# A two-layer trunk in fp32: tile work moved from GpSimd to VectorE and ScalarE, and the norms' full outputs kept for the seven products

## The chip, the cores and the metric

One Trainium2 chip, one of its cores. The time is the device time of one execution in microseconds; several executions of each kernel are timed, and the median counts. A trace of one profiled execution goes with it. The engines are named PE (TensorE, matrix products), DVE (VectorE), ACT (ScalarE), POOL (GpSimd) and SP (SyncE, which issues the transfers). "L162" is line 162 of the kernel before; the lines of the changed kernel lie up to five away.

## The reference

An encoder trunk of two layers on 512 tokens of 1024 features. Each layer has three steps, so there are six in all, n = 0 to 5; each ends in a residual and a layer norm:

```python
for i in range(DEPTH):
    mods = (cond @ ada_w[i] + ada_b[i]).reshape(b, N_SUB, 3, D_MODEL)
    gate = lambda s: (1 + mods[:, s, 2])[:, None, :]
    y = swiglu(modulate(x, mods[:, 0]), ffn_w_gate[i, 0], ffn_w_up[i, 0], ffn_w_down[i, 0])
    x = layer_norm(ALPHA * x + 0.5 * gate(0) * y, ln_g[i, 0], ln_b[i, 0])
    u = modulate(x, mods[:, 1])
    ...
    x = layer_norm(ALPHA * x + gate(1) * y, ln_g[i, 1], ln_b[i, 1])
    y = swiglu(modulate(x, mods[:, 2]), ffn_w_gate[i, 1], ffn_w_up[i, 1], ffn_w_down[i, 1])
    x = layer_norm(ALPHA * x + 0.5 * gate(2) * y, ln_g[i, 2], ln_b[i, 2])
```

The middle step is a bidirectional Mamba-2 scan in layer 0 (n = 1) and differential attention in layer 1 (n = 4); n = 0, 2, 3, 5 are SwiGLU feed-forward networks (FFN) of width 2816. `modulate(x, m)` is x * (1 + scale) + shift, where shift, scale and gate come from the condition vector through the large matrix ada_w.

## The kernel before, in words

**Layout.** Activations lie transposed: features on the 128 partitions, the 512 tokens along the free axis, so x is eight tiles res[0] to res[7] of 128x512 fp32.

**Products.** An fp32 product is made of three matmuls in a reduced format (`mm3`, L158 to L166; all show as L162): each factor is split into a rounded part and the remainder, and hi x hi, hi x lo and lo x hi are summed. Inputs are uh and ul (or hi and lo for the inner activations), weights wh and wl. `load` fetches 128x1024 of weights to one of four buffers (raw); `split` (L102 to L121) makes the rounded part on ACT (L119, or L110) and the remainder on DVE (L120). In the form "a" it makes two tiles wah and two tiles wal of 128x512 in the pool "a", which holds NA tiles; of the two wal (L112) POOL makes the first and DVE the second, except in the start, where DVE makes both.

**The norm** (class LN, L260 to L361). `start` estimates the mean of each token from the first 128 features by a matmul with z0 (L272) and takes the estimate m0 off all eight res tiles (L277: six on DVE, two on POOL). `feed` adds each tile, as its residual is done (L371, DVE), to a running sum sc (L292) and its square (ACT, L288) to ss (L293); both sums are POOL's, but where a tile comes late (`late`) the sc sums and the last ss sum are DVE's. `stats` reduces sc and ss over the partitions on PE (L299, L303), makes 1/std (small DVE steps, a power on POOL at L317), spreads it on PE (L249, the broadcast) and takes the rest of the mean off on DVE (L321). `normalize` multiplies by 1/std (L347, DVE), makes uh and a full copy lt on ACT (L349, two ACTIVATEs per tile), and ul = lt - uh on DVE (L350). lt is a scratch tile. The scalings of res for the next residual (`residual`, L357, ACT) wait in the list `later`.

**The end of a step** (`down_units`, L388 to L417). All but the last four output blocks (six in n = 1 and 4) are made for all tokens. The last ones are kept and made by token halves, 256 columns each: the statistics and the normalising of the first half run while PE makes the second half's blocks. While the second half's statistics and normalising run, PE can work on the next layer's first products for the first token half. Their weights, the first units (`first_units`, L378 to L386: two or three units of 128x1024), are split in the form "a".

**The FFN.** In n = 2, 3 and 5 the blocks from f = 4 on are made by a scheme with seven half-size products in place of eight (`seven`, L476). It needs sums and differences of the full fp32 inputs: `input_forms` (L426 to L445) rebuilds each full input tile as uh + ul (L431, eight adds in an FFN), forms four sums for each pair of tiles (L433 to L436) and splits them. This goes on during f = 0 to 3. FFN 0 makes its blocks the plain way; it makes the forms near its end (f = 18 to 21) too, with eight adds, and doesn't use them. Between the blocks a stream of ada products runs (L180, DVE: one 128x1024 product with its sum per unit, with its own load through raw).

**The start** (L1031 to L1059). For each of the eight tiles d: two ada products on DVE, the shift and scale columns, uh and a full copy on ACT (L1045), ul on DVE (L1047; POOL for d = 0), the scaling of res by ALPHA on POOL (L1051), and the split of a weight unit, in the form "a" for d < 6.

**What sets the order.** Each engine works its own instructions in one fixed order, and waits by semaphores. That order isn't the program's: a scheduler fills the engines from the program, within the buffers that the pools have. A tile that is claimed from a pool comes behind the pool's tiles that the program claimed ahead of it. SP issues the loads in order.

Of the kernel before, what the change touches and what calls it, by code (L numbers as in the profile page):

```python
# [17 lines left out]
KT = D // P  # L18
FT = 22
FPARTS = (8, 7, 7)  # L20
NA = 32
NE = 5
NG = 4
NST = 128
# [22 lines left out]
def hybrid_trunk(tc, xT, cb, par, cst, adaw, wgu, wdn0, wdn1, wdn2, wdt, win, wso, wqk, wv, wao, dist_in, dtp, lam_in, out):  # L47
# [17 lines left out]
    def tmp(name="tmp"):  # L65
        return tp.tile([P, T], F32, tag="t", name=name)
# [28 lines left out]

    extra = [None]
    behind = []
    first_split = [True]
    first_ln = [None]
    turn = [0]  # L100

    def split(raw, where=None):  # L102

        n = raw.shape[-1]
        if where == "a":
            hi, lo = [], []
            for o in range(0, n, T):
                r = raw[:, o : o + T]
                h, l = big(F32R, "wah"), big(F32R, "wal")
                x = nc.scalar.activation(h, r, AF.Copy)  # L110
                eng = nc.vector if first_split[0] or o else nc.gpsimd
                y = eng.tensor_tensor(out=l, in0=r, in1=h.bitcast(F32), op=ALU.subtract)  # L112
# [147 lines left out]
    class LN:  # L260
# [6 lines left out]
        def start(self):  # L267

            pm = acc("ln")
            z0 = tp.tile([P, T], F32R, tag="t", name="z0")  # L270
            nc.scalar.activation(z0, res[0], AF.Copy)
            nc.tensor.matmul(pm, lhsT=onesn, rhs=z0, start=True, stop=True)  # L272
            m0 = ap.tile([P, T], F32, tag="l", name="m0", bufs=3)
            nc.scalar.activation(m0, pm, AF.Copy)
            for d in range(KT):
                eng = nc.gpsimd if d >= 6 else nc.vector
                eng.tensor_tensor(out=res[d], in0=res[d], in1=m0, op=ALU.subtract)  # L277
# [3 lines left out]
        def feed(self, d, a, b, late=False):  # L281
            z = res[d][:, a:b]
            if d == 0:
                self.start()
                nc.scalar.activation(self.ss[:, a:b], z, AF.Square)
                return
            sq = sp.tile([P, T], F32, tag="sq", name="sq")
            nc.scalar.activation(sq[:, a:b], z, AF.Square)  # L288
            c0 = res[0] if d == 1 else self.sc
            e0 = nc.vector if late else nc.gpsimd  # L290
            e1 = nc.vector if late and d == KT - 1 else nc.gpsimd
            e0.tensor_tensor(out=self.sc[:, a:b], in0=c0[:, a:b], in1=z, op=ALU.add)  # L292
            e1.tensor_tensor(out=self.ss[:, a:b], in0=self.ss[:, a:b], in1=sq[:, a:b], op=ALU.add)  # L293

        def stats(self, a, b):
            n, m = self.n, (b - a) // P
# [27 lines left out]
        def normalize(self, a, b, rb):  # L324
            n = self.n
            if n == 5:
                for d in range(KT):
                    t = res[d][:, a:b]
                    nc.vector.scalar_tensor_tensor(
                        out=t, in0=t, scalar=pc(C_LNG + n * 8 + d), in1=rb, op0=ALU.mult, op1=ALU.mult  # L330
                    )
                    nc.scalar.activation(t, t, AF.Identity, bias=pc(C_LNB + n * 8 + d))
                    if d % 2:
                        nc.sync.dma_start(
                            out[(d - 1) * P : (d + 1) * P, a:b].rearrange("(e p) t -> p e t", e=2),
                            resid[:, d - 1 : d + 1, a:b],
                        )
                return
            if self.u is None:
                self.u = [  # L340
                    tuple(ap.tile([P, T], F32R, tag="u", name=x, bufs=2 * KT) for x in ("uh", "ul")) for _ in range(KT)
                ]
            for d in range(KT):
                G, B = lnG[n][:, d : d + 1], lnB[n][:, d : d + 1]
                z, t = res[d][:, a:b], tmp("lt")[:, a:b]
                uh, ul = self.u[d][0][:, a:b], self.u[d][1][:, a:b]
                nc.vector.tensor_tensor(out=z, in0=z, in1=rb, op=ALU.mult)  # L347
                for o in (uh, t):
                    nc.scalar.activation(o, z, AF.Identity, bias=B, scale=G)  # L349
                nc.vector.tensor_tensor(out=ul, in0=t, in1=uh.bitcast(F32), op=ALU.subtract)  # L350
# [22 lines left out]
            op0=ALU.mult, op1=ALU.add,  # L373
        )

    next_u = [None]

    def first_units(n):  # L378

# [8 lines left out]
    def down_units(n, u, units, last, KEEP=4):  # L388
# [15 lines left out]
        if last:  # L404
            rbs = []
            for a, b in HALVES:
                for d, w in keep:
                    pd = acc()
                    proj(pd, w, u, cols=((a, b),))
                    add_res(d, pd, n, a, b)  # L410
                    ln.feed(d, a, b, late=True)
# [11 lines left out]

    def input_forms(u):  # L426

        for k in range(4):
            top, bot = tmp("ft"), tmp("fb")
            for o, d in ((top, k), (bot, k + 4)):  # L430
                nc.vector.tensor_tensor(out=o, in0=u[d][0].bitcast(F32), in1=u[d][1].bitcast(F32), op=ALU.add)  # L431
# [75 lines left out]
    def ffn(n, stream=None, per=(0, 0), pre=None, first7=FT):  # L507
# [6 lines left out]
        u = next_u[0]  # L514
        f = 0
        pre = pre or first_units(n)
        for pi, nf in enumerate(FPARTS):
            hs = []
            open7 = None
            for _ in range(nf):  # L520
# [19 lines left out]
                nc.vector.tensor_tensor(out=h, in0=sg, in1=pu, op=ALU.mult)  # L540
                hs.append(split_act(h))
                if first7 - 4 <= f < first7:
                    making = making or input_forms(u)
# [490 lines left out]
    for d in range(KT):  # L1034
# [20 lines left out]
    first_split[0] = False  # L1055
    behind.clear()
    next_u[0] = up
    st0 = ada_stream(0, range(16, 72))
# [111 lines left out]
```

## Time and profile before

| | |
|---|---|
| median of 3 runs | 2225.82 us (2225.81 to 2229.15) |
| profiled execution, its time | 2227.95 us |
| its span in the trace | 2226.2 us |
| PE, DVE, ACT, POOL busy | 97%, 76%, 47%, 12% of the span |
| granted PE clock, mean | 0.991 |
| matmuls / DVE / ACT / POOL instructions | 13030 / 2850 / 1758 / 332 |
| HBM read, written | 289.53 MB, 5.24 MB |

The profile is read like this. The page gives each engine's busy time and what ended its waits; a group is a line, an engine, an operation and its tiles, with count, busy time, mean of one in ns, and the idle time ahead of it with the instruction that ended it. Stretches give busy times between two moments and the clock that PE was granted (1.00 is full speed). The timeline gives single instructions with start and length. Instructions of DVE and ACT overlap a little at their ends, so that the pitch from one start to the next may be shorter than the length shown. The norms' first statistics (the first L299) stand at 375.9, 825.8, 1194.1, 1556.2, 1847.9 and 2202.1 us for n = 0 to 5.

### The profile page before, as it was taken

Reading aid. Unit: us, or ns where it says so; the run is one execution under the profiler, and the core shown is the slowest. Engines: PE = TensorE matmul, PEld = TensorE weight load, DVE = VectorE, ACT = ScalarE, POOL = GpSimd, SP = SyncE. Lnnn points to the kernel's source line nnn. Section 1 sums busy time; section 2 is a strip of 40 time slices with the busy share of each in tenths; the row PEclk is TensorE's granted clock in tenths of the full one; section 3 lists DMA queues with packets and bytes.
Section 4 is the critical chain, followed back from the end, with each engine's and each line's share of the span. In section 5 each row is a group of like instructions: output and inputs, shape, how many; then the busy total and the mean of one; then the engine's idle time right before and its main releaser. Section 6 shows DMA issues by size and latency. Waiting matters only on the chain.

```text
span 2226.2 us, 33653 instructions
## 1 busy us (share of the span) xinstructions
PE 2161.8 (97%) x13030; PEld 1862.6 (84%) x13030; DVE 1697.3 (76%) x2850; ACT 1055.2 (47%) x1758; POOL 273.4 (12%) x332
## 2 busy tenths in 40 slices
PE   7999999999999989999999999999999999999998
PEld 5788888866777679889898989899877778989897
DVE  6865568556766689989888998897766679959696
ACT  4422234757656537434355534344755556425253
POOL 2000003035332330000003000003000012000003
PEclk9999999999999999999999999999999999999999
DMA  8865562375445423545542273733211122323231
GB/s 300 283 210 175 181 200 80 96 184 150 136 132 156 119 70 107 193 156 184 166 133 92 92 253 103 238 106 122 68 57 52 53 67 67 115 75 116 84 117 46
DMA packets 88545, 296.97 MB, mean 133 GB/s; under 512 B 9536, under 2 KB 12992, under 8 KB 88384
## 3 DMA queue, kind: packets, MB, share of 16 engines
q1 hardware_dynamic: 88384, 294.81, 41.8%
q8 instruction: 102, 1.67, 0.3%
q14 instruction: 59, 0.48, 0.1%
HBM read 289.53 MB, written 5.24 MB: 132 GB/s over the span
## 4 chain that ended last, share of the span: by engine, by line
PE 48%; DVE 9%; issue 4%; ACT 3%; DMA 2%; POOL 1%; POOLq 0%; ACTq 0%; DVEq 0%; SPq 0%
PE acc L162 38%; PE mid L162 6%; DVE wl L120 1%; DMA raw<-in_wdn 1%; PE mid L938 1%; DVE raw L464 1%; PE ln L162 1%; DVE wl L455 1%; DVE raw L180 1%; DVE lo L150 1%; PE ln L249 1%; DMA raw<-in_adaw 1%; ACT wh L119 1%; DVE resid L277 1%; DVE resid L371 0%
## 5 line engine op out<-in xcount | busy, mean ns | idle before, releaser
L162 PE MATMUL acc<-hi,wh 128*128 128x512 f32 (+1 forms) x1488 | 506.0, 341 | 9.8 <-DVE resid L371 6.7
L162 PE MATMUL acc<-hi,wl 128*128 128x512 f32 (+1 forms) x1488 | 505.9, 340 | 1.1 <-DVE wl L455 1.1
L162 PE MATMUL acc<-lo,wh 128*128 128x512 f32 (+1 forms) x1488 | 504.9, 339 | 0.0
L162 PE MATMUL acc<-uh,wh 128*128 128x512 f32 (+1 forms) x1256 | 441.6, 352 | 0.3 <-ACT wh L119 0.3
L162 PE MATMUL acc<-ul,wh 128*128 128x512 f32 (+1 forms) x1256 | 439.5, 350 | 0.2 <-DVE ul L1047 0.2
L162 PE MATMUL acc<-uh,wl 128*128 128x512 f32 (+1 forms) x1256 | 438.2, 349 | 0.8 <-DVE wl L120 0.8
L119 ACT ACTIVATE wh<-raw 128x1024 fp32r<-128x1024 f32 (+1 forms) x234 | 238.6, 1025 | 392.3 <-PE acc L162 199.1
L120 DVE TENSOR_TENSOR wl<-raw,wh 128x1024 fp32r<-128x1024 f32 (+1 forms) x234 | 281.2, 1202 | 81.1 <-ACT wh L119 71.3
L162 PEld LDWEIGHTS acc<-hi,wh 128*128 128x128 f32 x1488 | 283.8, 191 | 46.2 <-DVE resid L371 6.5
L162 PEld LDWEIGHTS acc<-hi,wl 128*128 128x128 f32 x1488 | 284.1, 191 | 32.2 <-DVE wl L455 1.5
L162 PEld LDWEIGHTS acc<-lo,wh 128*128 128x128 f32 x1488 | 283.9, 191 | 31.0 <-DVE lo L150 1.0
L162 PEld LDWEIGHTS acc<-uh,wh 128*128 128x128 f32 x1256 | 237.4, 189 | 40.2 <-issue 9.2
L454 ACT ACTIVATE wh<-raw 128x1024 fp32r<-128x1024 f32 x162 | 170.8, 1059 | 207.5 <-DVE raw L464 105.2
L162 PEld LDWEIGHTS acc<-uh,wl 128*128 128x128 f32 x1256 | 237.6, 189 | 35.0 <-issue 3.9
L162 PEld LDWEIGHTS acc<-ul,wh 128*128 128x128 f32 x1256 | 237.8, 189 | 33.7 <-issue 4.4
L180 DVE SCALAR_TENSOR_TENSOR raw<-raw,cond 128x1024 f32<-128x1024 f32 x144 | 176.9, 1235 | 55.8 <-DMA raw<-in_adaw 55.4
L455 DVE TENSOR_TENSOR wl<-raw,wh 128x1024 fp32r<-128x1024 f32 x162 | 196.9, 1219 | 27.1 <-ACT wh L454 26.1
L371 DVE SCALAR_TENSOR_TENSOR resid<-acc,gv,resid 128x512 f32<-128x512 f32 (+1 forms) x172 | 113.0, 659 | 78.5 <-PE acc L162 78.2
L464 DVE TENSOR_TENSOR raw<-raw 128x512 f32<-128x512 f32 x216 | 148.1, 689 | 4.4
L112 POOL TENSOR_TENSOR wal<-raw,wah 128x512 fp32r<-128x512 f32 x13 | 19.7, 1517 | 951.7 <-ACT wah L110 655.5
L162 PE MATMUL mid<-uh,wh 128*128 128x256 f32 (+2 forms) x332 | 94.7, 286 | 0.9 <-DVE up L496 0.9
L162 PE MATMUL mid<-uh,wl 128*128 128x256 f32 (+2 forms) x332 | 93.9, 283 | 0.0
(269 smaller groups left out, 3824.8 us busy)
## 6 DMA issues: line engine op xcount, KB each, us to landing
raw<-in_wgu SPq DMA_DIRECT2D x176, 512.0 KB, 3.9
raw<-in_adaw SPq DMA_DIRECT2D x144, 512.0 KB, 4.6
raw<-in_wdn SPq DMA_DIRECT2D x64, 448.0 KB, 3.7
raw<-in_win SPq DMA_DIRECT2D x40, 512.0 KB, 3.6
raw<-in_wdn SPq DMA_DIRECT2D x32, 512.0 KB, 4.5
rw<-scr SPq DMA_DIRECT2D x32, 512.0 KB, 5.4
ch<-scr SPq DMA_DIRECT2D x32, 256.0 KB, 3.5
raw<-in_wso SPq DMA_DIRECT2D x16, 512.0 KB, 3.5
```

The lines of the kernel that those rows point to most:

```text
L119: nc.scalar.activation(hi[:, :n], raw, AF.Copy)
L120: nc.vector.tensor_tensor(out=lo[:, :n], in0=raw, in1=hi[:, :n].bitcast(F32), op=ALU.subtract)
L150: y = nc.vector.tensor_tensor(out=lo, in0=src, in1=hi.bitcast(F32), op=ALU.subtract)
L162: last = nc.tensor.matmul(o, lhsT=a, rhs=b, start=start and j == 0, stop=j == n - 1, skip_group_check=not start)
L180: nc.vector.scalar_tensor_tensor(out=raw, in0=raw, scalar=1.0, in1=cond, op0=ALU.mult, op1=ALU.mult, accum_out=mods[l][:, j : j + 1],)
L249: nc.tensor.matmul(o[:, j * P : (j + 1) * P], lhsT=cols[:, j : j + 1].broadcast_to([P, P]), rhs=ident, start=True, stop=True)
L277: eng.tensor_tensor(out=res[d], in0=res[d], in1=m0, op=ALU.subtract)
L371: nc.vector.scalar_tensor_tensor(out=res[d][:, a:b], in0=pd[:, a:b], scalar=gvec[n][:, d : d + 1], in1=res[d][:, a:b], op0=ALU.mult, op1=A ...
L454: nc.scalar.activation(x[0], r, AF.Copy)
L455: nc.vector.tensor_tensor(out=x[1], in0=r, in1=x[0].bitcast(F32), op=ALU.subtract)
L464: nc.vector.tensor_tensor(out=o, in0=x, in1=y, op=ALU.add)
L938: nc.tensor.matmul(ss[m], lhsT=a[r, c], rhs=b[r, :], start=j == 0, stop=j == 2)
```

## The change

No tile work stays on POOL in the splits, the start, the feeds and the norms: the wal of the splits, the subtractions of the mean, the sc and ss sums and ul of d = 0 go to DVE, and the scaling by ALPHA in the start goes to ACT through the list `later`. (POOL keeps the small power at L317 and some work elsewhere.) In n = 1, 2 and 4, whose next step is an FFN with seven products, `normalize` writes the full tile not to scratch but to a kept tile "uf" of the pool "a", and `input_forms` works on it directly, without the adds of L431. The pool "a" grows from 32 to 35 tiles.

```diff
-NA = 32
+NA = 35
...
                 x = nc.scalar.activation(h, r, AF.Copy)
-                eng = nc.vector if first_split[0] or o else nc.gpsimd
-                y = eng.tensor_tensor(out=l, in0=r, in1=h.bitcast(F32), op=ALU.subtract)
+                y = nc.vector.tensor_tensor(out=l, in0=r, in1=h.bitcast(F32), op=ALU.subtract)
...
             for d in range(KT):
-                eng = nc.gpsimd if d >= 6 else nc.vector
-                eng.tensor_tensor(out=res[d], in0=res[d], in1=m0, op=ALU.subtract)
+                nc.vector.tensor_tensor(out=res[d], in0=res[d], in1=m0, op=ALU.subtract)
...
-            e0 = nc.vector if late else nc.gpsimd
-            e1 = nc.vector if late and d == KT - 1 else nc.gpsimd
-            e0.tensor_tensor(out=self.sc[:, a:b], in0=c0[:, a:b], in1=z, op=ALU.add)
-            e1.tensor_tensor(out=self.ss[:, a:b], in0=self.ss[:, a:b], in1=sq[:, a:b], op=ALU.add)
+            nc.vector.tensor_tensor(out=self.sc[:, a:b], in0=c0[:, a:b], in1=z, op=ALU.add)
+            nc.vector.tensor_tensor(out=self.ss[:, a:b], in0=self.ss[:, a:b], in1=sq[:, a:b], op=ALU.add)
...
+            if a == 0:
+                keep = n in (1, 2, 4)
+                self.full = [big(name="uf") if keep else None for _ in range(KT)]
+                next_full[0] = self.full if keep else None
             for d in range(KT):
                 G, B = lnG[n][:, d : d + 1], lnB[n][:, d : d + 1]
-                z, t = res[d][:, a:b], tmp("lt")[:, a:b]
+                z, t = res[d][:, a:b], (self.full[d] or tmp("lt"))[:, a:b]
...
-    def input_forms(u):
+    def input_forms(u, full):
...
         for k in range(4):
-            top, bot = tmp("ft"), tmp("fb")
-            for o, d in ((top, k), (bot, k + 4)):
-                nc.vector.tensor_tensor(out=o, in0=u[d][0].bitcast(F32), in1=u[d][1].bitcast(F32), op=ALU.add)
+            if full is not None:
+                top, bot = full[k], full[k + 4]
+            else:
+                top, bot = tmp("ft"), tmp("fb")
+                for o, d in ((top, k), (bot, k + 4)):
+                    nc.vector.tensor_tensor(out=o, in0=u[d][0].bitcast(F32), in1=u[d][1].bitcast(F32), op=ALU.add)
...
-        eng = nc.gpsimd if d == 0 else nc.vector
-        y = eng.tensor_tensor(out=hl[1], in0=uf, in1=hl[0].bitcast(F32), op=ALU.subtract)
+        y = nc.vector.tensor_tensor(out=hl[1], in0=uf, in1=hl[0].bitcast(F32), op=ALU.subtract)
...
-        nc.gpsimd.tensor_scalar(out=res[d], in0=res[d], scalar1=ALPHA, scalar2=None, op0=ALU.mult)
+        later.append(lambda d=d: nc.scalar.activation(res[d], res[d], AF.Copy, scale=ALPHA))
```

The instructions stand in another order after it. On PE, at the end of step 1 (the scan), where the second half's statistics are made; acc<-lo,wh and acc<-hi,wl are step 1's own last products, acc<-uh,wah, acc<-ul,wah and acc<-uh,wal those of FFN 2's first units. Before:

```order
L162 MATMUL acc<-hi,wl 128x256
L162 MATMUL acc<-uh,wah 128x256 x3
L162 MATMUL acc<-uh,wh 128x256
L299 MATMUL mid<-sc,onesd 128x256
L303 MATMUL ln<-invd,sc 128x1 x2
L303 MATMUL ln<-invd,ss 128x1 x2
L162 MATMUL acc<-ul,wah 128x256
L162 MATMUL acc<-uh,wal 128x256
L162 MATMUL acc<-uh,wah 128x256
L162 MATMUL acc<-ul,wah 128x256
L162 MATMUL acc<-uh,wal 128x256
```

and after:

```order
L160 MATMUL acc<-hi,wl 128x256
L294 MATMUL mid<-sc,onesd 128x256
L298 MATMUL ln<-invd,sc 128x1 x2
L298 MATMUL ln<-invd,ss 128x1 x2
L247 MATMUL ln<-csts,rr 128x128 x2
L160 MATMUL acc<-uh,wah 128x256
L160 MATMUL acc<-ul,wah 128x256
L160 MATMUL acc<-uh,wal 128x256
```

Before, four matmuls of the next FFN stand ahead of the statistics and 45 between them and the broadcast (ln<-csts,rr, L249, which comes behind the rows shown). After, the broadcast (now L247) follows the statistics directly, and the next FFN's matmuls come behind it.

On ACT, at the same place, the splits of the first units (wah, six tiles) before:

```order
L110 ACTIVATE wah_7287<-raw_7285 128x512
L110 ACTIVATE wah_7291<-raw_7285 128x512
L119 ACTIVATE wh_6908<-raw_6906 128x1024
L271 ACTIVATE z0_6866<-resid_88 128x512
L110 ACTIVATE wah_7297<-raw_7295 128x512
L274 ACTIVATE m0_6869<-ln_6865 128x512
L119 ACTIVATE wh_6914<-raw_6912 128x1024
L285 ACTIVATE ss_6880<-resid_88 128x512
L110 ACTIVATE wah_7301<-raw_7295 128x512
```

and after, first between the two halves' normalising (uh and uf), then at the end of it:

```order
L348 ACTIVATE uf_7182<-resid_88,lnB1_2254,lnG1_2252 128x256
L348 ACTIVATE uh_7173<-resid_88,lnB1_2254,lnG1_2252 128x256
L109 ACTIVATE wah_7279<-raw_7277 128x512
L348 ACTIVATE uh_7159<-resid_88,lnB1_2254,lnG1_2252 128x256
L348 ACTIVATE uf_7175<-resid_88,lnB1_2254,lnG1_2252 128x256
```

```order
L348 ACTIVATE uh_7173<-resid_88,lnB1_2254,lnG1_2252 128x256
L348 ACTIVATE uf_7182<-resid_88,lnB1_2254,lnG1_2252 128x256
L109 ACTIVATE wah_7283<-raw_7277 128x512
L356 ACTIVATE resid_88<-resid_88,lnab1_2259,lnag1_2257 128x512
L109 ACTIVATE wah_7289<-raw_7287 128x512
L356 ACTIVATE resid_88<-resid_88,lnab1_2259,lnag1_2257 128x512
L109 ACTIVATE wah_7293<-raw_7287 128x512
L117 ACTIVATE wh_7432<-raw_7430 128x1024
L109 ACTIVATE wah_7299<-raw_7297 128x512
```

Before, four of the six wah stand around the mean's estimate (z0, m0), ahead of all the normalising. After, the first stands behind the first half's 16 ACTIVATEs, and the others behind the second half's 16, in turn with the scalings of res (L356). Norms 2 and 4 show the same; norms 0 and 3 keep matmuls of the next step between the second statistics and the broadcast.

More of the change, by code (lines that the diff above doesn't have):

```diff
@@ L97, in hybrid_trunk @@
     behind = []
-    first_split = [True]
     first_ln = [None]
@@ L275, in start, with feed @@
             for d in range(KT):
-                eng = nc.gpsimd if d >= 6 else nc.vector
-                eng.tensor_tensor(out=res[d], in0=res[d], in1=m0, op=ALU.subtract)
+                nc.vector.tensor_tensor(out=res[d], in0=res[d], in1=m0, op=ALU.subtract)
             self.sc = ap.tile([P, T], F32, tag="l", name="sc", bufs=3)
             self.ss = ap.tile([P, T], F32, tag="l", name="ss", bufs=3)
-        def feed(self, d, a, b, late=False):
+        def feed(self, d, a, b):
             z = res[d][:, a:b]
@@ L374, in add_res @@
         )
-    next_u = [None]
+    next_u, next_full = [None], [None]
     def first_units(n):
@@ L410, in down_units @@
                     add_res(d, pd, n, a, b)
-                    ln.feed(d, a, b, late=True)
+                    ln.feed(d, a, b)
                 if rbs:
@@ L513, in ffn @@
         idx = {0: 0, 2: 1, 3: 2, 5: 3}[n]
-        u = next_u[0]
+        u, full = next_u[0], next_full[0]
         f = 0
@@ L542, in ffn @@
                 if first7 - 4 <= f < first7:
-                    making = making or input_forms(u)
+                    making = making or input_forms(u, full)
                     forms.append(next(making))
@@ L1054, in hybrid_trunk @@
     nc.sync.dma_start(csts, cst[:, : 2 * P].rearrange("p (j q) -> p j q", j=2))
-    first_split[0] = False
     behind.clear()
```

## The prediction

> **What bounds the kernel now.** I read the page first, then the busy times in chosen stretches, then groups of instructions, and last the timeline around the norms.
>
> ```profile
> PE 2161.8 (97%) x13030; PEld 1862.6 (84%) x13030; DVE 1697.3 (76%) x2850; ACT 1055.2 (47%) x1758; POOL 273.4 (12%) x332
> ```
>
> TensorE (PE) is busy for 97% of the span, so whatever the change does can only count where PE waits. The stretches tell where that is (columns: start and end, length, busy time of each engine, granted clock, DMA share, GB/s).
>
> ```profile
> 809.00:826.00 17.00, 13.34 (x93) 12.77 (x93) 15.71 (x22) 7.76 (x15) 12.85 (x11) 0.90 0.22 77
> 838.00:852.70 14.70, 13.77 (x105) 12.96 (x106) 14.11 (x42) 12.64 (x26) 0.71 (x1) 1.00 0.03 5
> 863.00:933.00 70.00, 68.62 (x509) 65.13 (x509) 68.75 (x114) 34.97 (x52) 0.00 (x0) 1.00 0.45 144
> 1167.00:1194.00 27.00, 22.79 (x143) 20.35 (x142) 25.72 (x28) 7.91 (x14) 18.29 (x13) 1.00 0.53 173
> 1193.80:1200.60 6.80, 6.54 (x29) 6.39 (x30) 4.00 (x14) 1.52 (x3) 0.74 (x2) 0.50 0.01 2
> 1209.40:1219.00 9.60, 9.45 (x78) 9.19 (x77) 8.62 (x29) 8.86 (x17) 0.71 (x1) 1.00 0.01 2
> 1533.50:1556.20 22.70, 22.67 (x143) 20.50 (x143) 16.36 (x21) 7.32 (x12) 14.77 (x11) 1.00 0.33 114
> 1830.00:1848.00 18.00, 13.91 (x95) 13.31 (x96) 16.67 (x23) 8.19 (x15) 12.65 (x10) 0.91 0.28 89
> 1859.00:1872.60 13.60, 13.57 (x112) 13.30 (x111) 12.87 (x38) 11.41 (x23) 0.86 (x2) 1.00 0.01 2
> 1880.00:1940.00 60.00, 60.00 (x458) 57.70 (x457) 57.62 (x95) 34.12 (x52) 0.00 (x0) 1.00 0.30 96
> 2100.00:2150.00 50.00, 50.00 (x416) 49.61 (x416) 43.71 (x67) 24.69 (x37) 0.00 (x0) 1.00 0.31 98
> ```
>
> Three things stand here. The last row is the steady state: 416 matmuls in 50 us, 0.12 us for one of 256 columns. The rows from 809, 1167 and 1830 are the first parts of norms 1, 2 and 4: PE idles 3.7, 4.2 and 4.1 us while DVE is nearly full (15.71 of 17, 25.72 of 27, 16.67 of 18) and POOL works beside it; the granted clock is 0.90 and 0.91 on the mean of the first and third, which is some 3.4 us at half speed, and 0.50 for 6.8 us behind the wait in norm 2. The rows from 838, 1209.4 and 1859 are the second halves of the same norms, and there PE is full: it works on the next layer's first units (wah and wal) while ACT and DVE normalise. This second overlap is what I think the change takes away.
>
> **The POOL work that goes to DVE.** The groups (mean ns after the busy time) price it.
>
> ```profile
> L277 DVE TENSOR_TENSOR resid<-resid,m 128x512 f32<-128x512 f32 x36 | 38.6, 1138 | 4.1 <-ACT m L274 4.1
> L431 DVE TENSOR_TENSOR fb<-uh,ul 128x512 f32<-128x512 f32 x16 | 10.9, 684 | 0.0
> L110 ACT ACTIVATE wah<-raw 128x512 fp32r<-128x512 f32 x38 | 22.0, 616 | 0.3 <-DMA raw<-in_wqk 0.3
> ```
>
> The same two-input DVE operation on 512 columns takes 1138 ns in L277, where POOL runs, and 684 ns in L431, where it doesn't. So DVE slows down for POOL's sake, and taking POOL's part over costs DVE less than it looks: 8 subtractions at 0.61 us (a pitch shown below) are 4.9 us, where 6 take 6 x 1.14 = 6.8. The Trainium skill ("SBUF — State Buffer", Who interferes with whom) says that a DVE instruction with two SBUF inputs contends with a GpSimd instruction that reads SBUF, whichever starts first holding the shared ports for a whole instruction. The two DVE rows agree; by that rule alone the first parts of the norms shorten and the total falls.
>
> How much sooner the first statistics come I worked out for norm 1, from rows of DVE in the start and in this norm (start, length; the pitch is from one start to the next).
>
> ```profile
> 18.57 1.10 DVE L112 TENSOR_TENSOR wal<-raw,wah 128x512 fp32r<-128x512 f32 x1
> ...
> 24.95 1.10 DVE L112 TENSOR_TENSOR wal<-raw,wah 128x512 fp32r<-128x512 f32 x1
> 25.97 1.21 DVE L180 SCALAR_TENSOR_TENSOR raw<-raw,cond 128x1024 f32<-128x1024 f32 x1
> ...
> 27.11 0.68 DVE L112 TENSOR_TENSOR wal<-raw,wah 128x512 fp32r<-128x512 f32 x1
> 27.72 1.21 DVE L180 SCALAR_TENSOR_TENSOR raw<-raw,cond 128x1024 f32<-128x1024 f32 x1
> ...
> 809.88 2.79 DVE L277 TENSOR_TENSOR resid<-resid,m 128x512 f32<-128x512 f32 x2 [2.02 <-ACT m L274]
> ...
> 820.58 0.47 DVE L371 SCALAR_TENSOR_TENSOR resid<-acc,gv,resid 128x256 f32<-128x256 f32 x1
> 820.98 0.56 DVE L292 TENSOR_TENSOR sc<-sc,resid 128x256 f32<-128x256 f32 x1
> ...
> 825.25 0.41 DVE L292 TENSOR_TENSOR sc<-sc,resid 128x256 f32<-128x256 f32 x1
> 825.59 1.48 DVE L293 TENSOR_TENSOR ss<-ss,sq 128x256 f32<-128x256 f32 x1
> ```
>
> The pitches are 0.61 for 512 columns (27.11 to 27.72), 1.14 for 1024 (25.97 to 27.11), 0.40 for a half-width residual (820.58 to 820.98), 0.34 for a half-width sum (825.25 to 825.59). After the change DVE has 8 x 0.61 for subtractions, 0.7 for one full residual, 1.14 for one wl, 2 x 0.61 for full sums, 6 x 0.40 and 12 x 0.34: 14.4 us. From 809.3 (half a microsecond sooner, an estimate: m0 no longer follows ACT work for the first units) that ends at 823.7, against 825.59 + 1.48 = 827.07 now: 3.4 us. I take 3.5. It could be no more than the 3.7 us of idle PE plus half of the 3.4 us at half clock, 5.4. In norm 2 the same ceiling is 4.2 + 3.4 = 7.6, in norm 4 it is 4.1 + 1.7 = 5.8. Between 0.65 of the ceiling, as in norm 1, and all of it I take 5.5 and 4.7; norm 2 in the lower part, because an ada product with its own load stands in its chain.
>
> **What the kept inputs move.** Each full tile uf is claimed from the pool that wah and wal use, ahead of them in the program. The order shows the effect: in norms 1, 2 and 4 the first wah stands behind all 16 normalising ACTIVATEs of the first half, the other five behind the 16 of the second half, and between the second half's statistics and the broadcast of 1/std PE has no next-layer matmul left (45, 17 and 45 of them before). Norms 0 and 3, which keep nothing, have their matmuls still there. After the broadcast PE can do what the first wah/wal pair allows, 12 matmuls (29 in norm 2, where a third product's 17 stand ahead too), and then waits for the second pair. When that is ready, R, follows from when the last normalising ACTIVATE of the second half ends now:
>
> ```profile
> 853.94 0.59 ACT L349 ACTIVATE uh<-resid,lnB,lnG 128x256 fp32r<-128x256 f32 x1
> 854.43 0.59 ACT L349 ACTIVATE lt<-resid,lnB,lnG 128x256 f32<-128x256 f32 x1
> ...
> 1222.68 0.59 ACT L349 ACTIVATE lt<-resid,lnB,lnG 128x256 f32<-128x256 f32 x1
> ...
> 1875.56 0.59 ACT L349 ACTIVATE lt<-resid,lnB,lnG 128x256 f32<-128x256 f32 x1
> ```
>
> Less the lead, plus 0.6 for wah (616 ns) and 0.6 for wal on DVE: R is 855.0 - 3.5 + 1.2 = 852.7 in norm 1, 1223.3 - 5.5 + 1.2 = 1219.0 in norm 2, 1876.15 - 4.7 + 1.2 = 1872.65 in norm 4. DVE arrives at the same moment: from the broadcast it has 16 half-width operations, six sums of the seven products that now stand among them, one ada product of 1.14 and two wal, 9.5 us, and ACT has 16 x 0.49 (853.94 to 854.43) + 1.2 = 9.0, a little after DVE's first product.
>
> What before has done by R, the windows that start with the second statistics count. 14 of each are the statistics' and the broadcast's own passes; 4, 14 and 4 next-layer matmuls stand ahead of the window. So it is 105 - 14 + 4 = 95, 78 - 14 + 14 = 78 and 112 - 14 + 4 = 102, against 12, 29 and 12: PE is behind by 83, 49 and 90 matmuls of 0.12 us, 10.0 + 5.9 + 10.8 = 26.7 us. After R the other pairs follow faster than PE eats them (24 matmuls, 2.9 us, for each pair; 1.5 us of ACT with a residual scaling between), so nothing more is lost.
>
> **The clock.** PE then idles several microseconds in each of the three norms. The half-speed stretches above followed such waits and lasted 3.4 or 6.8 us, which loses 1.7 or 3.4. I take 2.6 for each norm, 7.8.
>
> **The start.** In the rows of DVE above, one step of the chain (weight units of one d) takes 24.95 - 18.57 = 6.38 us. The wal beside POOL's scaling takes 1.10, the other 0.68; without POOL some 0.33 to 0.4 goes from each of six steps. ACT takes the eight scalings, between its wah's, where it waits for the chain anyway. I take -2.0 (between 6 x 0.4 = 2.4 and nothing).
>
> **The removed sums.** 24 of 32 adds of L431 go, 24 x 0.684 = 16.4 us of DVE. They stand in the first part of FFNs 2, 3 and 5, where PE is busy 68.62 of 70 us (863, FFN 2) and 60 of 60 (1880, FFN 5): PE hides them. I cost that at nothing; were the cover gone, it would be worth at most the 1.4 us of idle PE in the first of these. Norms 0, 3 and 5 lose POOL too, but there PE doesn't wait for DVE (1533.5, the first part of norm 3: PE 22.67 of 22.7, DVE 16.36); I take 0, at most -2 for the three. NA alone moves nothing in time.
>
> **The sum.** 26.7 + 7.8 - 2.0 = +32.5 us. On the profiled run (span 2226.2, run 2227.95) that is 2260.4; that run lies 2.1 above the median of 2225.82, so the forecast for the median is 2258.
>
> Its bounds: with leads of 2 us more in each norm (-6), no clock loss (-7.8), -0.4 in the start and -2 in the other norms it is +16; with half the leads (+6.9), 3.4 of clock in each norm (+2.4), a half-clock stretch more in norm 2 (+3.4) and no gain in the start (+2) it is +47. The forecast's own range is 2242 to 2273.
>
> **The rivals.** A: the freed DVE decides, the late splits are covered after all. For it speaks DVE's 1138 against 684 ns, against it PE's full rows from 838, 1209.4 and 1859, which no other work can fill. The gain is the leads and the start: 3.5 + 5.5 + 4.7 + 2.0 = 15.7, 2210. The Trainium skill ("GPSIMD Engine Reference", 4.1 Engine selection) would have it so: elementwise work on two tiles belongs on VectorE. Chance 0.05.
>
> B: slower only by the bare chain of the statistics, which the leads pay back. Norm 5 shows this chain with nothing in its way:
>
> ```profile
> 2212.87 0.28 PE L162 MATMUL acc<-hi,wl 128*128 128x256 f32 x1
> ...
> 2217.57 1.07 PE L249 MATMUL ln<-csts,rr 128*128 128x128 f32 x4 [1.90 <-POOL rr L317]
> ```
>
> 2217.57 - 2212.87 = 4.7 us. If PE went on at full pace right behind the broadcast, three norms would lose 14.1 and gain 13.7 + 2.0: 2224, no change. It decides if the second wah is ready with the broadcast, and the order of ACT speaks against that. Chance 0.07.
>
> C: more than forecast. The first units' loads keep three of four raw buffers until their splits, so the loads behind them come late as well. A load takes
>
> ```profile
> raw<-in_wgu SPq DMA_DIRECT2D x176, 512.0 KB, 3.9
> ```
>
> 3.9 us; two of them bare in each norm are 23, 2281. Against it: DMA is busy for 0.45 and 0.30 in the stretches from 863 and 1880, and PE has 144 matmuls, 17 us, to cover them. Chance 0.08.
>
> **How the numbers follow.** Forecast 0.80, A 0.05, B 0.07, C 0.08. A difference of 0.2%, 4.5 us, is about what a measurement of this kernel can tell. Faster 0.05 (A), same 0.07 (B), slower 0.88. The range reaches from a little below the forecast's own low end to C, 2236 to 2284; it leaves out A, B and the tails.
>
> **What would show it.** In the profile after, PE should idle twice in norms 1, 2 and 4: from the second statistics to the broadcast (some 5 to 6 us), and, after 12 matmuls (29), until the second wal; the granted clock should read 0.50 behind it. L277's subtractions on DVE should take some 0.65 us, and the first statistics come 3 to 5 us sooner in the norm. The beginnings of FFNs 2, 3 and 5 should stay full. It is wrong if PE has next-layer matmuls in that gap, if those norms take no longer than before, or if the loss is spread over the FFNs.

## The result and the profile after

The changed kernel takes 2250.51 us (median of 4 runs, 2245.99 to 2253.47), the kernel before 2227.49 on the same chips; the ratio is 1.0102, 95% interval 1.0081 to 1.0122. It is slower by some 23 us, where the forecast had 32.5 (2258); the time lies inside the range on record. The profiled run took 2250.82 us, its span 2249.0, 22.8 us more than the span before. The rows below are of that run, where no other is named.

First the page's engines, then stretches with the columns as before: the first part of norm 1; norm 1 from the second statistics to the broadcast, from there until the second wal, and a little on; the beginning of FFN 2; then norm 2 and norm 4 from the second statistics on, two stretches each, and a longer one behind the broadcast of norm 4.

```profile
PE 2164.1 (96%) x13030; PEld 1866.4 (83%) x13030; DVE 1689.1 (75%) x2924; ACT 1060.3 (47%) x1766; POOL 133.5 (6%) x226
```

```profile
803.00:818.40 15.40, 13.44 (x104) 12.81 (x104) 14.46 (x31) 5.27 (x10) 0.00 (x0) 1.00 0.14 49
828.50:835.00 6.50, 2.28 (x10) 2.10 (x10) 6.19 (x21) 6.50 (x14) 0.69 (x1) 0.54 0.02 4
835.00:846.90 11.90, 5.22 (x18) 4.13 (x18) 11.67 (x33) 10.92 (x23) 0.00 (x0) 0.50 0.12 44
846.90:849.50 2.60, 2.60 (x13) 2.54 (x13) 2.60 (x8) 2.60 (x5) 0.00 (x0) 0.51 0.54 200
858.00:928.00 70.00, 70.00 (x536) 67.25 (x535) 55.73 (x84) 32.94 (x49) 0.00 (x0) 1.00 0.39 129
1205.50:1210.20 4.70, 1.50 (x11) 1.37 (x11) 4.60 (x17) 4.70 (x11) 0.69 (x1) 0.75 0.00 2
1210.20:1219.60 9.40, 4.86 (x19) 4.08 (x19) 9.08 (x25) 8.53 (x18) 0.00 (x0) 0.50 0.00 0
1863.80:1870.40 6.60, 1.50 (x11) 1.37 (x11) 6.29 (x21) 6.60 (x14) 0.70 (x1) 0.71 0.00 0
1870.40:1882.00 11.60, 4.98 (x18) 4.09 (x18) 11.38 (x31) 10.62 (x22) 0.00 (x0) 0.50 0.15 46
1870.40:1892.00 21.60, 14.98 (x81) 13.83 (x82) 20.15 (x48) 20.47 (x36) 0.00 (x0) 0.61 0.36 119
```

In the second halves, where PE was full before, it now does 10 or 11 matmuls (the statistics' own) in 4.7 to 6.6 us, and some 18 in the next 9 to 12 us, while DVE and ACT are nearly full. The granted clock falls to 0.50 within the first stretch of each norm and stays there through the second. The beginning of FFN 2 is as full as it was (70 of 70; 68.62 before), with DVE at 55.73 in place of 68.75 us.

The timeline of PE in norm 1 (start, length, idle time and what ended it) shows the waits and what ended them; the last row is the power on POOL:

```profile
828.50 0.79 PE L294 MATMUL mid<-sc,onesd 128*128 128x256 f32 x2 [2.55 <-DVE sc L287]
...
835.05 1.22 PE L247 MATMUL ln<-csts,rr 128*128 128x128 f32 x4 [4.27 <-POOL rr L312]
836.72 0.58 PE L160 MATMUL acc<-uh,wah 128*128 128x256 f32 x1 [0.45 <-ACT wah L109]
...
841.83 0.58 PE L160 MATMUL acc<-uh,wal 128*128 128x256 f32 x1 [4.32 <-DVE wal L110]
...
846.19 0.58 PE L160 MATMUL acc<-uh,wah 128*128 128x256 f32 x1 [1.86 <-ACT wah L109]
```

```profile
834.30 0.69 POOL L312 TENSOR_TENSOR rr<-vr,mhalf 128x2 f32<-128x2 f32 x1 [12.71 <-DVE vr L308]
```

PE waits 4.27 us for the power on POOL with nothing else to do. The power itself takes 0.69; most of the wait is DVE's, whose small steps ahead of the power (up to 834.13) stand among the normalising of the first half. PE then does two matmuls with the first wah, waits 4.32 us for the first wal, does the ten that are left of the twelve, and waits 1.86 us for the second wah. That one comes on ACT right behind the last normalising ACTIVATE (uf at 845.04), and its wal on DVE ends at 846.91. The third row of DVE below is the second wal of norm 4, which ends at 1882.23. The weights are not what is late: SP issued the loads of the first two units from 799.13 on, they took some 3.4 us to land, and the first wah begins at 836.06.

```profile
799.13 2.08 SPq L93 DMA_DIRECT2D raw<-in_wgu  x2
```

```profile
836.06 0.61 ACT L109 ACTIVATE wah<-raw 128x512 fp32r<-128x512 f32 x1
...
845.04 0.58 ACT L348 ACTIVATE uf<-resid,lnB,lnG 128x256 f32<-128x256 f32 x1
845.53 0.61 ACT L109 ACTIVATE wah<-raw 128x512 fp32r<-128x512 f32 x1
```

```profile
841.10 0.68 DVE L110 TENSOR_TENSOR wal<-raw,wah 128x512 fp32r<-128x512 f32 x1
...
846.23 0.68 DVE L110 TENSOR_TENSOR wal<-raw,wah 128x512 fp32r<-128x512 f32 x1
...
1881.55 0.68 DVE L110 TENSOR_TENSOR wal<-raw,wah 128x512 fp32r<-128x512 f32 x1
```

Where the time came from is read by the same instruction in both runs. The remainder of the inner activations (L150, in the changed kernel L148) runs 192 times in either; the 1st, 46th, 71st, 106th, 111th, 161st and 181st lie in the first FFN, just ahead of norm 1, in FFN 2, at the end of FFN 3 (ahead of norm 3), in the attention behind norm 3, ahead of norm 4 and in FFN 5. Before:

```profile
63.54 0.68 DVE L150 TENSOR_TENSOR lo<-h,hi 128x512 fp32r<-128x512 f32 x1
802.53 1.13 DVE L150 TENSOR_TENSOR lo<-yn,hi 128x512 fp32r<-128x512 f32 x1
1114.64 0.69 DVE L150 TENSOR_TENSOR lo<-sg,hi 128x512 fp32r<-128x512 f32 x1
1529.34 0.69 DVE L150 TENSOR_TENSOR lo<-sg,hi 128x512 fp32r<-128x512 f32 x1 [0.70 <-ACT hi L149]
1609.19 0.69 DVE L150 TENSOR_TENSOR wtl<-ln,wth 128x512 fp32r<-128x512 f32 x1
1814.59 0.69 DVE L150 TENSOR_TENSOR wtl<-ln,wth 128x512 fp32r<-128x512 f32 x1 [0.18 <-ACT wth L149]
2028.09 0.68 DVE L150 TENSOR_TENSOR lo<-sg,hi 128x512 fp32r<-128x512 f32 x1
```

and after:

```profile
59.89 0.68 DVE L148 TENSOR_TENSOR lo<-h,hi 128x512 fp32r<-128x512 f32 x1
797.25 0.68 DVE L148 TENSOR_TENSOR lo<-yn,hi 128x512 fp32r<-128x512 f32 x1
1118.41 0.68 DVE L148 TENSOR_TENSOR lo<-sg,hi 128x512 fp32r<-128x512 f32 x1
1538.98 0.69 DVE L148 TENSOR_TENSOR lo<-sg,hi 128x512 fp32r<-128x512 f32 x1 [0.70 <-ACT hi L147]
1618.24 0.68 DVE L148 TENSOR_TENSOR wtl<-ln,wth 128x512 fp32r<-128x512 f32 x1
1823.69 0.69 DVE L148 TENSOR_TENSOR wtl<-ln,wth 128x512 fp32r<-128x512 f32 x1 [0.18 <-ACT wth L147]
2050.59 0.68 DVE L148 TENSOR_TENSOR lo<-sg,hi 128x512 fp32r<-128x512 f32 x1
```

The differences are -3.65, -5.28, +3.77, +9.64, +9.05, +9.10 and +22.50 us. So the start gained 3.7 and the way to norm 1 another 1.6; norm 1, with the beginning of FFN 2, cost 9.1, norm 2, with FFN 3, cost 5.9, norm 3 gave 0.6 back, and norm 4 cost 13.4. The three norms that keep their outputs make the whole loss, 28.3 us.

### The profile page after: what moved, and what is told of

Same layout as the page of the kernel before. It is cut to its first block, busy times and chain, and to the rows that moved or that the text cites. A ratio compares the mean times of both kernels' runs of the same rounds, so it can differ in the third digit from the quotient of the medians.

```text
span 2249.0 us, 33533 instructions
## 1 busy us (share of the span) xinstructions
PE 2164.1 (96%) x13030; PEld 1866.4 (83%) x13030; DVE 1689.1 (75%) x2924; ACT 1060.3 (47%) x1766; POOL 133.5 (6%) x226
## 4 chain that ended last, share of the span: by engine, by line
PE 76%; DVE 10%; ACT 4%; issue 4%; DMA 3%; POOL 2%; POOLq 0%; ACTq 0%; SPq 0%; DVEq 0%
PE acc L160 63%; PE mid L160 7%; DMA raw<-in_adaw 2%; DVE raw L178 1%; DVE raw L467 1%; PE mid L941 1%; DMA raw<-in_wdn 1%; POOL E L780 1%; PE ln L160 1%; DVE wl L118 1%; DVE wl L458 1%; PE mid L791 1%; ACT uh L348 1%; PE ln L247 1%; ACT uf L348 1%
## 5 line engine op out<-in xcount | busy, mean ns | idle before, releaser
L312 POOL TENSOR_TENSOR rr<-vr,mhalf 128x2 f32<-128x2 f32 x12 | 8.4, 696 | 1580.4 <-DVE vr L308 1219.3
```

## Experiments

The theory is that the claims make the loss: uf is claimed from the pool "a" ahead of wah and wal, so the splits of the next FFN's first units come behind the normalising, and PE has nothing to do meanwhile. Rival 1 is that the work moved from POOL to DVE costs; rival 2 that the kept tiles cost as such, whoever claims first. Ratios are to the kernel before on the same chip, with 95% intervals.

### The first units claimed ahead of the kept tiles (claim)

```diff
                 keep = n in (1, 2, 4)
+                if keep:
+                    next_pre[0] = first_units(n + 1)
                 self.full = [big(name="uf") if keep else None for _ in range(KT)]
...
-        pre = pre or first_units(n)
+        pre, next_pre[0] = pre or next_pre[0] or first_units(n), None
```

> The changed kernel with one edit: the first units of the next FFN are claimed ahead of the kept tiles uf. Theory (the order of the claims): the splits stand around the mean's estimate again, PE has 33, 27 and 43 next-layer matmuls between the second statistics and the broadcast in norms 1, 2 and 4, the 28 us that these norms lost (9.0 + 6.0 + 13.4) go, and the earlier statistics count as gain: 2206 to 2216. Rival 1 (the work moved to DVE is what costs): 2245 to 2255, as the change. Rival 2 (kept tiles and raw buffers, whoever claims first): 2235 to 2250.

Measured: 2211.29 us, ratio 0.9934 (0.9919 to 0.9949). The same changed kernel with the claims exchanged is 0.7% faster than the kernel before, not 1% slower. Between the second statistics and the broadcast, and on, PE is full in norms 1 and 4:

```profile
828.80:837.50 8.70, 8.65 (x44) 8.35 (x45) 8.31 (x26) 6.89 (x15) 0.90 (x1) 0.61 0.41 123
1839.40:1849.00 9.60, 9.60 (x53) 9.42 (x54) 9.17 (x28) 8.36 (x17) 0.69 (x1) 0.64 0.18 55
```

The clock means of 0.61 and 0.64 are what is left of a wait ahead of the second statistics, to which the run claim_ss2 comes back. This kernel keeps the 35 tiles, the moved work and the kept tiles, so rivals 1 and 2 fall as causes of the loss. It shows that the order decides with the room unchanged; whether a larger pool would free the splits in the old order, no run tells.

The rows of the remainders say where the gain lies. Against before, claim is 4.2 us ahead in the start, 6.2 ahead of norm 1 and 8.0 in FFN 2, but 15.2 at the end of FFN 3, and hardly more behind it (15.8 in FFN 5; the profiled run of before is itself 2.1 us over its median). So about half of the gain comes in norm 2, where before PE waits 3.65 us for the first statistics and then runs 6.8 us at half clock. In claim the wait is 0.66 and the clock stays at 1.00. The 71st and 106th remainder in claim, and the wait before and in claim:

```profile
1106.68 0.69 DVE L148 TENSOR_TENSOR lo<-sg,hi 128x512 fp32r<-128x512 f32 x1
1514.19 0.69 DVE L148 TENSOR_TENSOR lo<-sg,hi 128x512 fp32r<-128x512 f32 x1 [0.70 <-ACT hi L147]
```

```profile
1194.06 1.19 PE L299 MATMUL mid<-sc,onesd 128*128 128x256 f32 x2 [3.65 <-DVE sc L292]
```

```profile
1182.74 0.70 PE L294 MATMUL mid<-sc,onesd 128*128 128x256 f32 x2 [0.66 <-DVE sc L287]
```

### No kept tiles, only the moved work (no_keep)

```diff
-NA = 35
+NA = 32
...
-                keep = n in (1, 2, 4)
+                keep = False
```

> The changed kernel without the kept tiles (no uf, the adds of input_forms back, 32 tiles in the pool); only the work of POOL has moved. Theory: within 3 us of the run with the claims exchanged, 2206 to 2218, since the 16.4 us of adds lie under a full PE. Rival 1 (moved work costs): 2245 to 2255. A second rival, that the removed adds do count: slower than the run with the claims exchanged by more than 5 us.

Measured: 2211.96 us, ratio 0.9941 (0.9925 to 0.9956). It can't be told from the run before it: with or without the 24 adds, the time is the same.

### Only the kept tiles (keep_only)

The kernel before with `keep`, the tiles uf and `input_forms(u, full)` as in the change; all POOL work stays.

```diff
-NA = 32
+NA = 35
...
+            if a == 0:
+                keep = n in (1, 2, 4)
+                self.full = [big(name="uf") if keep else None for _ in range(KT)]
+                next_full[0] = self.full if keep else None
...
```

> The kernel before with the kept tiles alone, claimed ahead of the first units (35 tiles in the pool); POOL keeps its work. PE has 0, 0 and 2 next-layer matmuls between second statistics and broadcast. Theory: the loss without the gains of the start (3.7) and of the earlier statistics: slower than the changed kernel, 2254 to 2270. Rival 1: no loss, 2224 to 2230. Rival 2 (kept tiles as such): 2240 to 2250.

Measured: 2258.46 us, ratio 1.0142 (1.0122 to 1.0162), slower than the changed kernel. Norm 1 has the same hole, with POOL at work behind it:

```profile
836.10:842.80 6.70, 1.49 (x11) 1.35 (x11) 6.38 (x22) 6.45 (x14) 0.71 (x1) 0.64 0.01 2
842.80:860.00 17.20, 12.92 (x81) 11.75 (x82) 16.90 (x40) 16.39 (x31) 5.64 (x3) 0.84 0.33 107
```

### The kept tiles with the claims exchanged, POOL as before (keep_claim)

Both edits above, on the kernel before.

> The kernel before with the kept tiles, the first units claimed ahead of them; POOL keeps its work. This is the value of the 24 removed adds alone. Theory: nothing, 2223 to 2229. If the adds counted: 2210 to 2220. Rival 2 (kept tiles and raw buffers): 2235 or more.

Measured: 2225.0 us, ratio 1.0004 (0.9993 to 1.0014). 16.4 us of DVE work less is worth nothing: PE hides it. With these four runs the change falls into two parts. The moved work is worth 0.6% (no_keep), the kept tiles nothing where they are claimed late (keep_claim against before, claim against no_keep), and 1.4 to 1.7% of loss where they are claimed early (keep_only against before; the change, 1.0102, against claim, 0.9934).

### Where the moved work gains: the start alone (start_only)

```diff
-        eng = nc.gpsimd if d == 0 else nc.vector
-        y = eng.tensor_tensor(out=hl[1], in0=uf, in1=hl[0].bitcast(F32), op=ALU.subtract)
+        y = nc.vector.tensor_tensor(out=hl[1], in0=uf, in1=hl[0].bitcast(F32), op=ALU.subtract)
...
-        nc.gpsimd.tensor_scalar(out=res[d], in0=res[d], scalar1=ALPHA, scalar2=None, op0=ALU.mult)
+        later.append(lambda d=d: nc.scalar.activation(res[d], res[d], AF.Copy, scale=ALPHA))
```

> The kernel before with the start alone changed: the scaling by ALPHA on ACT, ul of the first tile on DVE. Theory: 6 steps of the chain shorter by 0.6 each, as the changed kernel's trace shows: 3.0 to 4.3 us less than before, ratio 0.9981 to 0.9987. Rival (the norms that follow wait as long as they did and give it back): within 1 us of before.

Measured: 2221.85 us, ratio 0.9990 (0.9980 to 1.0000). The span of its profiled run is 2220.9, 5.3 us under that of before. The interval holds the theory and reaches into the rival's range, so the timing doesn't settle it. The traces speak for the theory: the first remainder comes 4.2 us sooner in this run and the 46th, ahead of norm 1, still 3.3 us sooner (3.65 and 5.28 in the change).

### Two subtractions back on POOL (claim_sub)

On the kernel of the run claim:

```diff
             for d in range(KT):
-                nc.vector.tensor_tensor(out=res[d], in0=res[d], in1=m0, op=ALU.subtract)
+                eng = nc.gpsimd if d >= 6 else nc.vector
+                eng.tensor_tensor(out=res[d], in0=res[d], in1=m0, op=ALU.subtract)
```

> The kernel with the claims exchanged, with two of the eight subtractions of the mean back on POOL. Theory (DVE is slowed while POOL reads): 6 x 1.14 in place of 8 x 0.61 us, 1.9 us later in each of norms 1, 2 and 4, and a longer wait of PE there: 2213 to 2219; the group on DVE reads 1.0 to 1.2 us. Rival (DVE as such is the limit, so that POOL's help pays): 2204 to 2210, the group reads some 0.65.

Measured: 2215.99 us, ratio 0.9963 (0.9951 to 0.9976), outside the interval of claim (0.9919 to 0.9949). DVE does six subtractions in place of eight and is later for it. The group in this run, and in the changed kernel:

```profile
L275 DVE TENSOR_TENSOR resid<-resid,m 128x512 f32<-128x512 f32 x36 | 31.0, 926 | 1.5 <-ACT m L272 1.5
```

```profile
L274 DVE TENSOR_TENSOR resid<-resid,m 128x512 f32<-128x512 f32 x48 | 29.4, 683 | 5.4 <-ACT m L272 5.4
```

926 ns each with POOL's two beside them, 683 without POOL, 1138 in the kernel before, where POOL made a wal there too in four of the norms. 31.0 us for 36 are more than 29.4 for all 48. I had expected 1.0 to 1.2 us, and the mean mixes two cases. In norms 0, 1, 4 and 5 the six on DVE took 5.9 us together and POOL's two 3.1 to 3.5. In norms 2 and 3 the six took 3.69, the pace without POOL, and POOL's two 7.1. One of the two engines gives way, not always DVE, and these runs don't show what decides it.

### All sums of the feeds as before (claim_feed)

On the kernel of claim:

```diff
-            nc.vector.tensor_tensor(out=self.sc[:, a:b], in0=c0[:, a:b], in1=z, op=ALU.add)
-            nc.vector.tensor_tensor(out=self.ss[:, a:b], in0=self.ss[:, a:b], in1=sq[:, a:b], op=ALU.add)
+            e0 = nc.vector if late else nc.gpsimd
+            e1 = nc.vector if late and d == KT - 1 else nc.gpsimd
+            e0.tensor_tensor(out=self.sc[:, a:b], in0=c0[:, a:b], in1=z, op=ALU.add)
+            e1.tensor_tensor(out=self.ss[:, a:b], in0=self.ss[:, a:b], in1=sq[:, a:b], op=ALU.add)
...
```

> The kernel with the claims exchanged, with all sums of the feeds as in the kernel before (POOL, and DVE where a tile comes late). Theory: the first parts of norms 1, 2 and 4 wait for POOL's sums again and lose part of what the change won there, the second halves gain as in the run before this one: 2208 to 2218. Rival (the feeds made the whole gain of the moved work beside the start): 2218 to 2224.

Measured: 2217.64 us (2210.45 to 2224.09), ratio 0.9980 (0.9966 to 0.9994). The value is at the upper end of what the theory said and 0.4 us under the rival's range; the interval reaches into both, so the time alone doesn't part them. The trace bears out the theory: PE waits for the first statistics of norms 1, 2 and 4 again, 2.17, 1.97 and 2.17 us, where in claim it waits 0.66 us in norm 2 alone.

### The first wal of each pair on POOL (claim_wal)

On the kernel of claim:

```diff
-                y = nc.vector.tensor_tensor(out=l, in0=r, in1=h.bitcast(F32), op=ALU.subtract)
+                eng = nc.vector if first_split[0] or o else nc.gpsimd
+                y = eng.tensor_tensor(out=l, in0=r, in1=h.bitcast(F32), op=ALU.subtract)
```

> The kernel with the claims exchanged, with the first wal of each pair back on POOL. Theory: DVE is spared two or three wal of 0.6 us in each of norms 1, 2 and 4 but is slowed for 1.5 us at a time while POOL reads: within 4 us of the kernel with the claims exchanged, 2208 to 2215; no wal but one stands ahead of the second half's last sums on DVE. Rival (moving the wal made the gain of the change): 2216 to 2222.

Measured: 2214.84 us, ratio 0.9961 (0.9948 to 0.9973), within what the theory said; the interval touches that of claim, and the rival's range begins 1.2 us higher. Undone, each of the three moves costs a little (0.3 to 0.5% against claim, with intervals of some 0.15% to either side of each ratio). Together that is 1.0%, more than the 0.7% of all the moved work, so the three can't be added up; no single one makes the whole gain.

### A wait that the moved work leaves (claim_ss2)

In norms 1 and 4 of claim PE waits for the second statistics. I took the sums of squares on DVE for the cause and gave them back to POOL:

```diff
-            nc.vector.tensor_tensor(out=self.ss[:, a:b], in0=self.ss[:, a:b], in1=sq[:, a:b], op=ALU.add)
+            e1 = nc.gpsimd if a and d < KT - 1 else nc.vector
+            e1.tensor_tensor(out=self.ss[:, a:b], in0=self.ss[:, a:b], in1=sq[:, a:b], op=ALU.add)
```

> The kernel with the claims exchanged, with the sums of squares of the second token half (all but the last tile's) back on POOL. In norms 1 and 4 of that kernel PE waits 2.9 and 2.3 us for the second statistics, behind DVE, and runs 6.8 us at half clock after it. Theory (these sums on DVE made that wait): the wait falls under 1 us and the half clock goes in both norms, 2 x (2 + 3) us: 2199 to 2206. Rival (DVE loses as much to POOL's reads as it is spared): 2208 to 2214.

Measured: 2208.96 us, ratio 0.9939 (0.9925 to 0.9953), the same as claim; the theory of this run fails and its rival holds. In claim the wait of PE and the end of DVE's chain are

```profile
828.85 1.06 PE L294 MATMUL mid<-sc,onesd 128*128 128x256 f32 x2 [2.73 <-DVE sc L287]
```

```profile
827.38 0.47 DVE L372 SCALAR_TENSOR_TENSOR resid<-acc,gv,resid 128x256 f32<-128x256 f32 x1
827.78 0.68 DVE L110 TENSOR_TENSOR wal<-raw,wah 128x512 fp32r<-128x512 f32 x1
828.38 0.41 DVE L287 TENSOR_TENSOR sc<-sc,resid 128x256 f32<-128x256 f32 x1
```

and in this run

```profile
825.99 0.70 PE L295 MATMUL mid<-sc,onesd 128*128 128x256 f32 x2 [2.27 <-DVE sc L287]
```

```profile
824.16 0.84 DVE L287 TENSOR_TENSOR sc<-sc,resid 128x256 f32<-128x256 f32 x1
824.92 0.68 DVE L110 TENSOR_TENSOR wal<-raw,wah 128x512 fp32r<-128x512 f32 x1
825.52 0.41 DVE L287 TENSOR_TENSOR sc<-sc,resid 128x256 f32<-128x256 f32 x1
```

The wait fell by 0.5 us only: a wal of 0.6 stands ahead of the last sum in both, and beside POOL the sum ahead of it takes 0.84 in place of 0.41. In norm 4 it didn't fall (2.11 in claim, 2.22 here).

### The first units claimed sooner still (claim_early)

So I moved the claim ahead of the step's last blocks, which takes all of norm 1's wal out of that place:

```diff
         keep = []
+        if last and n in (1, 2, 4):
+            next_pre[0] = first_units(n + 1)
```

> The kernel with the claims exchanged, with the first units claimed still sooner, before the last step's output blocks. All six wal of norm 1 then stand on DVE around the subtractions of the mean, none between the second half's last residual and its last sum. Theory (in norms 1 and 4 a wal of 0.6 us and the sums behind which the last residual waits make the wait of PE ahead of the second statistics): that wait gets shorter (from 2.9 and 2.3 to about 1.5 to 2.3 us), but three more wal (1.8 us) come ahead of the first statistics, where DVE is the limit: 2207 to 2216. Rival (all that counts is that the splits are early): 2200 to 2207.

Measured: 2216.41 us, ratio 0.9963 (0.9951 to 0.9975), slower than claim. The trace shows both sides of the theory: the wait ahead of the second statistics of norm 1 falls from 2.73 to 1.80 us, but counted from the remainder ahead of each norm the first statistics come 0.6, 1.6 and 0.6 us later in norms 1, 2 and 4, and the wait in norm 4 grows from 2.11 to 2.77. Claiming early isn't good in itself; the splits have to stand where DVE has room. None of these edits beats claim. It can't be told from no_keep, which does without the kept tiles, nor from claim_ss2.

## Why the prediction was right

**The order.** That the claims delay the first units' splits, and that PE idles for it, is shown by claim and keep_only, in both directions. R, when the second pair is ready, was put at 852.7 in norm 1, 1219.0 in norm 2 and 1872.65 in norm 4, in the times of before. Measured: 846.91 in norm 1, and, with the run 5.28 us ahead there, 852.2. In norm 2 the second wal ends at 1221.78, less 3.8 it is 1218.0; in norm 4 at 1882.23, less 9.1 it is 1873.1. The way there was partly another. The prediction had PE do the first pair's 12 matmuls at once and then wait; it did two, waited over 4 us for the first wal on DVE in each of the three norms, and did the rest then. In norms 1 and 4 that changes nothing, since it still waited 1.86 us for the second pair. In norm 2 it didn't wait for that pair any more.

**The norms.** Predicted with the clock 12.6, 8.5 and 13.4, together 34.5; measured 9.1, 5.9 and 13.4, together 28.3. Norm 4 is right, and norms 1 and 2 are mis-sized by 3.5 and 2.6.

**The clock.** I took 2.6 us a norm. The clock did fall, but PE was mostly idle while it was low, and only the rest behind R counts: in norm 1 from 846.9 to 849.5, at half speed, 1.3 us. In norm 4 the mean of 0.61 in 21.6 us from 1870.4 is 16.8 us at half speed, to 1887.2, so some 5 us behind R: 2.5. In norm 2 PE is full from 1219.56 on with the third product, and the clock is low to 1221.5, so some 1.0. So 1.3 of the 3.5 us in norm 1 and 1.6 of the 2.6 in norm 2 are the clock. In norm 2 the other 1.0 is R, which came that much sooner. In norm 1 R came 0.5 us sooner, and PE did two matmuls with the second wah ahead of R, 0.2. The rest came behind the norm: 4149 matmuls are done by 870.0 us before and by 875.0 after, 4388 by 906.0 and by 909.2. So 5.0 us of lag have become 3.2 (3.8 from FFN 2's middle on): the norm itself cost 10.3, and the beginning of FFN 2 gave 1.2 back. By the same counts no_keep gains 1.1 us there and keep_claim 1.8, the one with the adds and the other without, so the removed adds are not the only way to it. Some 0.3 us of the 3.5 stay open.

**The start.** Predicted -2.0, seen -3.65, and 1.6 more until norm 1, which I hadn't in the sum; norm 3 gave 0.6, put at nothing. Together with the norms' 6.2 these are 10.0, and 0.3 us of loss behind the 181st remainder leave the 9.7 between 32.5 and 22.8.

**The lead.** For norm 1, 3.5 us. By the second statistics (838.0 before, 828.50 after, less 5.28) it was 4.2. But it was worked out for the first statistics, which were to come 3 to 5 us sooner in the norm. They stand at 818.44, 1193.49 and 1854.11 in norms 1, 2 and 4; less the lag ahead of each norm that is 2.1, 4.3 and 2.9 us sooner, so this sign held in norm 2 alone. The beginning of FFN 3 is a little less full than before, too (72.81 of 74 us from 1232; 74.00 from 1226 before); those of FFNs 2 and 5 are not.

**The removed sums** were put at nothing, and keep_claim shows just that, 1.0004 (0.9993 to 1.0014). Rival A had the right price for the moved work by luck: 2210, against 2211.29 in claim. Its parts are off: by the remainders claim gains 4.2 us in the start (2.0 in A), 2.0 on the way to norm 1 (nothing in A), and 1.8, 7.2 and 0.4 in norms 1, 2 and 4 (3.5, 5.5 and 4.7 in A). As a forecast A failed because the late splits weren't covered. B failed on the two waits behind the broadcast (4.32 and 1.86 us). C failed as FFN 2 began full. The rule of the Trainium skill's "SBUF — State Buffer" (Who interferes with whom), that a DVE instruction with two SBUF inputs contends with a GpSimd instruction that reads SBUF, is borne out by claim_sub: 926 ns on the mean for one operation with POOL at work beside it, 683 without.

## What to carry to other kernels

A tile that is kept longer has to be claimed from somewhere, and where a scheduler fills a pool in the program's order, whatever is claimed behind it in the same pool moves with it: compare what stands between the critical waits before and after, not only the room. Work taken off an engine that is hidden is worth nothing, here 16.4 us of it; work given to a second engine may slow the first by more than it saves, here 36 operations in 31.0 us against 48 in 29.4. An edit that bundles two changes can hide a gain of 0.7% in a net loss of 1%: time the parts.

## What the runs showed of the hardware

In the changed kernel the clock was low once in each of norms 1, 2 and 4, for 20.4, 13.6 and 20.4 us:

```profile
829.00:849.40 20.40, 9.50 (x38) 8.19 (x38) 19.86 (x58) 19.42 (x38) 0.69 (x1) 0.50 0.14 51
1207.90:1221.50 13.60, 6.79 (x27) 6.00 (x28) 13.20 (x38) 12.73 (x25) 0.69 (x1) 0.50 0.07 18
1866.70:1887.10 20.40, 10.09 (x40) 8.95 (x41) 20.03 (x55) 19.42 (x37) 0.70 (x1) 0.50 0.20 67
```

That is three, two and three times the 6.8 us for which it was low in norm 2 before. When it fell doesn't follow from the last wait alone. In norm 1 it fell 0.5 us behind a wait of 2.55; in norm 4 a wait of 2.37 left it at 1.00, and it fell 1.3 us into the next. The price is not the length but what PE has to do in it: in norm 1, behind R, 1.3 us of the 20. (The broadcast, which R waits for, took 1.22 us at half speed, against 0.71 at full speed in norm 2's first half, so up to 0.5 more may lie in R itself.)
